# A two-block sequence model on one core: later places for three groups of matrix products in the mixers

## Chip, core and metric

The kernel runs on 1 core of one Trainium2 chip. The metric is the device time of one execution in microseconds; lower is better.

## What is computed

Two blocks on a sequence of 256 tokens of width 1024. Only the first part of the first block matters here, its two mixers and the merge behind them:

```python
hn = rms_norm(h, norm_mix_pre)
p_rw, p_ret, g_rw, g_ret = _split(hn @ w_in, IN_SIZES)
y_rw  = rwkv7_mixer(p_rw, ...)      # 8 heads of 64, a state per head, sequential over the tokens
y_ret = retention_mixer(p_ret, positions)   # q, k rotated; v, gate; chunks of 128 tokens
merged = sigmoid(g_rw) * (y_rw @ w_branch_rw) + sigmoid(g_ret) * (y_ret @ w_branch_ret)
h = h + rms_norm(merged @ w_out, norm_mix_post)
```

In the recurrent mixer r, k, v, a decay and a gate come from projections of `hn` that are mixed with the previous token. k is normalised per head (`kk / max(sqrt(sum(kk*kk)), 1e-12)`), and the state takes one step per token. In the retention mixer q and k go through a rotary embedding, a group norm per head follows, and the result is multiplied by `silu(g)`.

## The kernel before

All products with a weight matrix are made in fp32 from a high and a low part: `mm3` (L257) issues three MATMULs (L258 to L260) for each pair of tiles. A weight tile of 128x1024 comes by DMA into one of 3 `raw` buffers; ScalarE (ACT) writes the high part `whi` (L254), VectorE (DVE) the low part `wlo` (L255). Both have 3 buffers (tag `w`), so a split waits until TensorE (PE) has used the weight three places before it.

`weave` (L130) runs two generators by turns: for every `yield` of the main one, `ratio` steps of the side one. The main one is `ret_qk`, `ret_vg`, `gates(0, 4)` (L825): the retention mixer and the first gates. Its projections (`gemm_a_block`, L525) yield after each 6 MATMULs of 128x512. The side one is `mixer` (L820): `features` (L434), with `RATIO0` = 1.2 steps per yield of the main one, then `rwkv` (L628) with 0.6.

`features` makes four features f = 0 to 3 of the recurrent mixer, two heads each, in 7 steps. `rw_feature(i, out)` (L394) is one projection: 24 MATMULs of 128x256, then an ACTIVATE (L403) and a DVE operation (L404). For one feature:

- `rw_feature(4 + f, km)` gives k. ACT scales and squares it (L442, L443); two small products and Tanh (L448, L449) give the decay, a scan (L452) its running sum.
- *norm step* (L455 to L464): two products with a 128x2 constant (L457) sum the squares, DVE (L459), POOL (`pow`, L296) and ACT (L461) make the factors `rn`, ACT two exponentials `e2`, `cs` (L462, L463).
- *key step* (L466 to L480): PE turns `rn` (L468), and a chain on DVE, with ACT's L471 and L472 in it, writes the two halves of `KB` (L469, L470, L473, L474, four of L478 and L479). `rw_feature(f, rm)` is issued behind it.
- *Gram step*: r times decay into `KR` (L482), 8 products `KB` x `KR` (L487), masked by DVE into `Gm` (L490), three transposes (L494).
- `rw_feature(8 + f, vm)`, then transposes of v (L503 to L505), ones-product of r*k (L512), bonus (L513).

`rwkv` first inverts four triangular matrices at once (`inverse`, L603; products L598, masked copies on DVE L618, L619), then goes through 4 chunks of 64 tokens; after chunks 1 and 3 a group norm follows (L694 to L704, again with `pow` on POOL), then transposes (L708), a product for the gate (L712) and the split of the result `yrT`.

`ret_vg` (L722) ends in `gated` (L781): a projection of 48 MATMULs, then for both token tiles t Tanh (ACT L789), two DVE operations (L790, L791) and four transposes (L285) into `ytT`. The merge loop (L859) makes, for each of 8 output tiles f, 24 MATMULs with `ytT` and 12 with `yrT`.

The sequence of the Python text isn't yet that of the engines: the framework's list scheduler orders the instructions of each engine at build time, by the text's order and by when it expects each to be ready. At run time each engine takes its instructions strictly in that order.

Of the kernel before, what the change touches and what calls it, by code (L numbers as in the profile page):

```python
# [114 lines left out]
YR, PB0, PB2, PA0, PA2 = 1, 2, 1, 2, 1  # L115
QL0, QL1, QL2 = 3, 1, 4

RATIO0, RATIO1, RATIO2, RATIO3, RATIO4, RATIO5, RATIO6 = 1.2, 0.6, 0.8, 0.55, 0.75, 0.8, 0.5


@with_exitstack
def tile_block(ctx: ExitStack, tc: tile.TileContext, io):
# [39 lines left out]
    def sm():  # L162
        return tl(qp, [P, 512], "sm", 4)
# [15 lines left out]
    def PR(name):  # L179
        lo, hi = PAR[name]  # L180
        return par[:, lo:hi]
# [212 lines left out]
    def rw_feature(i, out):  # L394

        ps = mm()
        if len(w_first) == 3:
            gemm_b_passes(ps[:, :T], w_first.pop(0), xT)
        else:
            gemm_b(ps[:, :T], w_first.pop(0) if w_first else rw.next(), xT)  # L400
        m = u2()
        G.memset(m[:, 0:1], 0.0)
        S.activation(out=m[:, 1:T + 1], in_=ps[:, :T], func=AF.Identity, scale=PR("mu")[:, i:i + 1])  # L403
        V.scalar_tensor_tensor(out=out, in0=ps[:, :T], scalar=omu[:, i:i + 1], in1=m[:, 0:T], op0=mult, op1=add)  # L404
# [20 lines left out]
    def c4(ap):  # L425
        return ap.rearrange("p (c l) -> p c l", c=4)
# [7 lines left out]
    def features():  # L434
        for f in range(4):
# [1 line left out]
            km, rm = duo()  # L437
            vm = bonus[f]
            rw_feature(4 + f, km)
            yield  # L440
            kk, sq = duo()
            S.activation(out=kk, in_=km, func=AF.Identity, scale=PR("kk")[:, fs])  # L442
            S.activation(out=sq, in_=kk, func=AF.Square)  # L443
# [8 lines left out]
            V.tensor_tensor_scan(out=cs, data0=C("scan64"), data1=ld, initial=0.0, op0=mult, op1=add)  # L452
            rn = ld
            yield
            pn = sm()  # L455
            for t in range(2):
                PE.matmul(pn[:, 2 * t:2 * t + 2], sq[:, t * P:(t + 1) * P], C("heads2"), start=True, stop=True)  # L457
# [4 lines left out]
            S.activation(out=e2, in_=cs, func=AF.Exp, scale=-1.0)  # L462
            S.activation(out=cs, in_=cs, func=AF.Exp)  # L463
            V.tensor_copy(out=PL[:, f, :], in_=c4(cs)[:, :, 63])  # L464
            yield
            pn = sm()  # L466
            for t in range(2):
# [8 lines left out]
            for x in range(2):  # L476
                b = slice(64 * x, 64 * x + 64)
                V.scalar_tensor_tensor(out=KB[b, :, 1 - x, :], in0=c4(kk)[b], scalar=0.5, in1=c4(e2)[b], op0=mult, op1=mult)  # L478
                V.tensor_tensor(out=KB[b, :, x, :], in0=c4(km)[b], in1=c4(e2)[b], op=mult)  # L479
            rw_feature(f, rm)  # L480
            yield
            V.tensor_tensor(out=KR[f][:, :, 1, :], in0=c4(rm), in1=c4(cs), op=mult)  # L482
            pgs = [sm(), sm()]
            for c in range(4):

# [8 lines left out]
                PE.transpose(pk[:, c * P:(c + 1) * P], KB[:, c].rearrange("p a l -> p (a l)"), ident)  # L494
            S.activation(out=KBn[:, f], in_=pk[:, 0:384].rearrange("p (c l) -> p c l", c=3), func=AF.Copy)
            yield
            rw_feature(8 + f, vm)
            yield


            pv, pw0 = sm(), sm()
# [5 lines left out]
            S.activation(out=VU[0:64, f, :, 0:64], in_=pv[0:64].rearrange("p (c l) -> p c l", c=4)[:, :, 0:64], func=AF.Copy)  # L507
            S.activation(out=VU[64:128, f, 1:4, 64:128], in_=pv3[64:128, :, 64:128], func=AF.Copy)
            S.activation(out=VU[64:128, f, 0, 64:128], in_=pw0[64:128, 0:64], func=AF.Copy)
            V.scalar_tensor_tensor(out=rm, in0=rm, scalar=PR("rk")[:, fs], in1=km, op0=mult, op1=mult)  # L510
            pb = sm()
            PE.matmul(pb[:, 0:T], C("ones2"), rm, start=True, stop=True)  # L512
            V.tensor_tensor(out=vm, in0=pb[:, 0:T], in1=vm, op=mult)  # L513
# [208 lines left out]
    def ret_vg():  # L722
# [58 lines left out]
        def gated():  # L781
            for b in range(2):
                outs = [mm(), mm()]
                yield from gemm_a_block(ret, xT, outs)
                while len(ocs) < 2:
                    yield
                for t in range(2):
                    th, z = ru(), ocs[t][:, b * 512:(b + 1) * 512]
                    S.activation(out=th, in_=outs[t], func=AF.Tanh, scale=0.5)  # L789
                    V.scalar_tensor_tensor(out=th, in0=th, scalar=1.0, in1=outs[t], op0=add, op1=mult)  # L790
                    V.tensor_tensor(out=z, in0=z, in1=th, op=mult)  # L791
                    transposes(z, 4, ytT, t, 4 * b)
                    yield
        yield from woven(gated(), outputs(), RATIO2)

# [26 lines left out]
        ratio[0] = RATIO1  # L822
        yield from rwkv()

    weave(chain(ret_qk(), ret_vg(), gates(0, 4)), mixer(), ratio)  # L825

    def down(acc, w, xT, k, first, last, ts=(0, 1)):

# [31 lines left out]
    pend = None  # L860
    for f in range(KD + 1):
        if f < KD:
            pb = mm()
            br, bt = halves(pb)
            wt_, wr_ = w_br.next(), w_br.next()
            gemm_b(bt, wt_, ytT)
            gemm_b(br, wr_, yrT, nk=4)
            tg = tgs[f]
            V.scalar_tensor_tensor(out=tg, in0=tg, scalar=1.0, in1=pb, op0=add, op1=mult)
            mf = tl(p1, [P, T], "Pn", 3)  # L870
            V.tensor_tensor(out=mf, in0=tg[:, 0:T], in1=tg[:, T:2 * T], op=add)
            if f < 4:
                mg = tl(p1, [P, 2, T], "qkT", 4, F32R)
            else:
                if f == 4:
                    kbn = tl(p1, [P, 4, 3, P], "KBn", 1, F32R).rearrange("p f c l -> p (f c l)")
                    bon = [tl(p1, [P, T], f"bonus{x}", 1, F32R) for x in range(2)]
                mg = kbn[:, (f - 4) * 512:(f - 3) * 512].rearrange("p (a l) -> p a l", a=2) if f < 7 else None
            mh, ml = (mg[:, 0, :], mg[:, 1, :]) if f < 7 else bon
            S.activation(out=mh, in_=mf, func=AF.Copy, scale=0.5)  # L880
            V.scalar_tensor_tensor(out=ml, in0=mf, scalar=0.5, in1=mh.bitcast(F32), op0=mult, op1=sub)
            for _ in gates(f + 4, min(f + 5, KD)):
                pass
            if EARLY <= f < EARLY + LATE1:
                w_late.append(w_l.next(spare[f - EARLY]))
        if pend is not None:
            k, x = pend
            if acc is None:
                acc = [[sm(), sm()], [sm(), sm()]]
            if k < KD - LATE1:  # L890
                down(acc, w_o.next(), x, k, k == 0, False)
            else:
                late.append((w_late[k - KD + LATE1], x, False))
        if f < KD:
            pend = (f, (mh, ml))
# [754 lines left out]
```

## Time and profile before

| | |
|---|---|
| runs (3) | 891.41, 894.54, 895.50 us, median 894.54 |
| the profiled execution | 894.72 us, its span 893.0 us |
| granted TensorE clock | 0.997 of full speed over the span |
| PE, DVE, ACT, POOL busy | 859.5, 649.8, 519.3, 70.7 us |

Reading it: the span goes from the first to the last instruction. PE means the MATMULs; their ends are modelled, so a row of busy PE can hide a fraction of a microsecond of waiting. An idle time in brackets behind a row, with an arrow, names what ended it. DMA moved 144 MB.

### The profile page before, as it was taken

The page shows a single profiled execution, that of the slowest core. Times are in us where ns is not written, and L with a number is a line of the kernel's source. Part 1 is how long each engine was busy: PE and PEld are TensorE (multiplying, and loading weights), DVE is VectorE, ACT ScalarE, POOL GpSimd, SP SyncE. Part 2 cuts the span into 40 slices and gives each one's busy share as a digit, 9 for nine tenths or more (in the row PEclk, how much of TensorE's full clock was granted, in tenths as well). Part 3 has the DMA queues.
Part 4 walks back from the last instruction along what each step waited for, and adds up shares of the span by engine and source line. Part 5 has one row for each costly group of instructions (what it writes and reads, how often), then busy time and mean ns, then how long its engine had stood idle before and what let it go on. Part 6 is the DMA issues. An engine that isn't in the chain of part 4 may idle for free.

```text
span 893.0 us, 15886 instructions
## 1 busy us (share of the span) xinstructions
PE 859.5 (96%) x6226; PEld 750.0 (84%) x6226; DVE 649.8 (73%) x1117; ACT 519.3 (58%) x933; POOL 70.7 (8%) x105
## 2 busy tenths in 40 slices
PE   9999999999999999999999899999999999999997
PEld 6788788789898889989999689978887888878776
DVE  7778865774755777888788848878786569867643
ACT  6555533454554556665566646668676467756652
POOL 2000000100100100000000100001101002402000
PEclk9999999999999999999999999999999999999999
DMA  8432431334566476655556435654534458543311
GB/s 278 144 136 99 130 131 66 105 105 147 172 218 207 165 243 215 226 180 197 188 177 207 150 103 200 226 201 146 189 120 140 160 175 285 171 170 108 116 36 36
DMA packets 41996, 144.44 MB, mean 162 GB/s; under 512 B 4977, under 2 KB 5569, under 8 KB 41922
## 3 DMA queue, kind: packets, MB, share of 16 engines
q1 hardware_dynamic: 41312, 141.32, 47.2%
q0 software_dynamic: 608, 2.11, 0.8%
q8 instruction: 49, 0.80, 0.4%
q14 instruction: 25, 0.20, 0.1%
q10 hardware_dynamic: 2, 0.00, 0.0%
HBM read 140.24 MB, written 3.18 MB: 161 GB/s over the span
## 4 chain that ended last, share of the span: by engine, by line
PE 39%; issue 22%; DVE 15%; DMA 14%; ACT 7%; POOL 3%; ACTq 0%; POOLq 0%; DVEq 0%; SPq 0%
PE mm L260 9%; PE mm L258 9%; PE mm L259 9%; DMA raw<-in_w_down 8%; DVE wlo L255 3%; PE sm L598 3%; ACT lhi L254 2%; DMA raw<-in_w_br 2%; DVE llo L255 2%; DMA raw<-in_w_up 1%; PE sm L285 1%; PE sm L1521 1%; ACT whi L254 1%; DVE elo L255 1%; POOL sg L1180 1%
## 5 line engine op out<-in xcount | busy, mean ns | idle before, releaser
L254 ACT ACTIVATE whi<-raw 128x1024 fp32r<-128x1024 f32 (+1 forms) x125 | 128.4, 1029 | 114.6 <-PE mm L259 38.4
L255 DVE TENSOR_TENSOR wlo<-raw,whi 128x1024 fp32r<-128x1024 f32 (+1 forms) x124 | 146.5, 1185 | 56.2 <-ACT whi L254 54.0
L258 PE MATMUL mm<-xTh,whi 128*128 128x256 f32 x616 | 174.8, 284 | 0.2 <-ACT xTh L254 0.2
L259 PE MATMUL mm<-xTl,whi 128*128 128x256 f32 x616 | 174.0, 283 | 0.3 <-DVE xTl L255 0.3
L260 PE MATMUL mm<-xTh,wlo 128*128 128x256 f32 x616 | 173.6, 282 | 0.4 <-DVE wlo L255 0.4
L259 PEld LDWEIGHTS mm<-xTl,whi 128*128 128x128 f32 x616 | 116.5, 189 | 2.4 <-issue 0.7
L258 PEld LDWEIGHTS mm<-xTh,whi 128*128 128x128 f32 x616 | 116.3, 189 | 2.3 <-ACT xTh L254 0.5
L260 PEld LDWEIGHTS mm<-xTh,wlo 128*128 128x128 f32 x616 | 116.2, 189 | 1.3 <-DVE wlo L255 0.9
L258 PE MATMUL mm<-whi,xTh 128*128 128x512 f32 x168 | 68.3, 407 | 0.0
L260 PE MATMUL mm<-whi,xTl 128*128 128x512 f32 x168 | 67.4, 401 | 0.0
L259 PE MATMUL mm<-wlo,xTh 128*128 128x512 f32 x168 | 66.1, 394 | 0.0
L258 PE MATMUL mm<-lhi,xTh 128*128 128x512 f32 (+1 forms) x156 | 61.4, 394 | 2.4 <-DVE xs L1064 1.9
L260 PE MATMUL mm<-lhi,xTl 128*128 128x512 f32 (+1 forms) x156 | 61.0, 392 | 0.0
L259 PE MATMUL mm<-llo,xTh 128*128 128x512 f32 (+1 forms) x156 | 60.2, 386 | 0.0
L255 DVE TENSOR_TENSOR llo<-raw,lhi 128x1024 fp32r<-128x1024 f32 x38 | 47.3, 1246 | 16.2 <-ACT lhi L254 15.7
L254 ACT ACTIVATE lhi<-raw 128x1024 fp32r<-128x1024 f32 x38 | 40.0, 1057 | 25.7 <-DMA raw<-in_w_down 16.9
L990 DVE SCALAR_TENSOR_TENSOR fc<-mm,par,fc 128x255 f32<-128x255 f32 x88 | 41.9, 477 | 7.8 <-ACT fc L987 7.3
L260 PE MATMUL mm<-xTh,elo 128*128 128x256 f32 x168 | 47.3, 281 | 0.0
L259 PE MATMUL mm<-xTl,ehi 128*128 128x256 f32 x168 | 47.3, 281 | 0.0
L258 PE MATMUL mm<-xTh,ehi 128*128 128x256 f32 x168 | 47.3, 281 | 0.0
L987 ACT ACTIVATE fc<-mm,par 128x256 f32<-128x256 f32 x44 | 24.3, 553 | 23.6 <-DVE fc L990 23.6
L990 DVE SCALAR_TENSOR_TENSOR cv<-mm,par,cv 128x255 f32<-128x255 f32 (+2 forms) x72 | 34.2, 475 | 4.7 <-ACT cv L987 4.0
(482 smaller groups left out, 2024.6 us busy)
## 6 DMA issues: line engine op xcount, KB each, us to landing
raw<-in_w_up SPq DMA_DIRECT2D x44, 512.0 KB, 4.0
raw<-in_w_xbc SPq DMA_DIRECT2D x25, 512.0 KB, 3.9
raw<-in_w_ret SPq DMA_DIRECT2D x24, 512.0 KB, 3.6
raw<-in_w_down SPq DMA_DIRECT2D x22, 512.0 KB, 4.6
raw<-in_w_gate SPq DMA_DIRECT2D x16, 512.0 KB, 3.5
raw<-in_w_z SPq DMA_DIRECT2D x16, 512.0 KB, 4.1
raw<-in_w_so SPq DMA_DIRECT2D x16, 512.0 KB, 4.4
raw<-in_w_pg SPq DMA_DIRECT2D x16, 512.0 KB, 4.3
```

Of the source, the lines that this page charges most:

```text
L254: first = S.activation(out=hi, in_=src, func=AF.Copy)
L255: last_split[:] = first.ins, (eng or V).tensor_tensor(out=lo, in0=src, in1=hi.bitcast(F32), op=sub).ins
L258: PE.matmul(out, sh, mh, start=start, stop=False)
L259: PE.matmul(out, sh, ml, start=False, stop=False)
L260: return PE.matmul(out, sl, mh, start=False, stop=stop).ins
L285: last = PE.transpose(ps[:, i, :], src[:, (j + i) * P:(j + i + 1) * P], ident)
L598: PE.matmul(fv(px)[u, f, :], lhsT(f, x), rhs[u, f, :], start=True, stop=True)
L987: S.activation(out=c, in_=ps, func=AF.Identity, scale=wv[:, (ntap - 1) * nf + i:(ntap - 1) * nf + i + 1], bias=bv[:, i:i + 1])
L990: V.scalar_tensor_tensor(out=c[:, d:], in0=ps[:, :T - d], scalar=wv[:, j:j + 1], in1=c[:, d:], op0=mult, op1=add)
L1180: G.affine_select(out=sg, in_=sg, pattern=[[0, 8], [1, P]], compare_op=ALU.is_ge, fill=NEG, base=0, channel_multiplier=-1)
L1521: PE.matmul(po[:, o:o + 64], eT[:, j * P:(j + 1) * P], vn[kb][:, kv * 64:(kv + 1) * 64], start=(kb == 0), stop=(kb == nk - 1))
```

## The change

In `features` the steps are cut anew. `rw_feature(f, rm)` moves from behind the key step to a step of its own behind the scan, ahead of the norm step. `rw_feature(8 + f, vm)` moves from behind the Gram step to the end of the key step. L482 (now L466) goes into the norm step, the product for the bonus (L510, now L483) into the key step. An empty step (a second `yield`) stands between norm and key step; a feature has 8 steps in place of 7, and `RATIO0` goes from 1.2 to 1.37. In `gated` the transposes come one `yield` after the DVE operations of both token tiles. A new generator `first_branches` puts the 24 `ytT` products of the first two merged tiles at the end of the main generator; the merge loop then adds their 12 `yrT` products. No instruction is added or taken away in these stages.

```diff
@@ -115,7 +115,7 @@
 YR, PB0, PB2, PA0, PA2 = 1, 2, 1, 2, 1
 QL0, QL1, QL2 = 3, 1, 4
 
-RATIO0, RATIO1, RATIO2, RATIO3, RATIO4, RATIO5, RATIO6 = 1.2, 0.6, 0.8, 0.55, 0.75, 0.8, 0.5
+RATIO0, RATIO1, RATIO2, RATIO3, RATIO4, RATIO5, RATIO6 = 1.37, 0.6, 0.8, 0.55, 0.75, 0.8, 0.5
 
 
 @with_exitstack
@@ -437,7 +437,6 @@
             km, rm = duo()
             vm = bonus[f]
             rw_feature(4 + f, km)
-            yield
             kk, sq = duo()
             S.activation(out=kk, in_=km, func=AF.Identity, scale=PR("kk")[:, fs])
             S.activation(out=sq, in_=kk, func=AF.Square)
@@ -452,6 +451,8 @@
             V.tensor_tensor_scan(out=cs, data0=C("scan64"), data1=ld, initial=0.0, op0=mult, op1=add)
             rn = ld
             yield
+            rw_feature(f, rm)
+            yield
             pn = sm()
             for t in range(2):
                 PE.matmul(pn[:, 2 * t:2 * t + 2], sq[:, t * P:(t + 1) * P], C("heads2"), start=True, stop=True)
@@ -462,6 +463,8 @@
             S.activation(out=e2, in_=cs, func=AF.Exp, scale=-1.0)
             S.activation(out=cs, in_=cs, func=AF.Exp)
             V.tensor_copy(out=PL[:, f, :], in_=c4(cs)[:, :, 63])
+            V.tensor_tensor(out=KR[f][:, :, 1, :], in0=c4(rm), in1=c4(cs), op=mult)
+            yield
             yield
             pn = sm()
             for t in range(2):
@@ -477,9 +480,9 @@
                 b = slice(64 * x, 64 * x + 64)
                 V.scalar_tensor_tensor(out=KB[b, :, 1 - x, :], in0=c4(kk)[b], scalar=0.5, in1=c4(e2)[b], op0=mult, op1=mult)
                 V.tensor_tensor(out=KB[b, :, x, :], in0=c4(km)[b], in1=c4(e2)[b], op=mult)
-            rw_feature(f, rm)
-            yield
-            V.tensor_tensor(out=KR[f][:, :, 1, :], in0=c4(rm), in1=c4(cs), op=mult)
+            V.scalar_tensor_tensor(out=rm, in0=rm, scalar=PR("rk")[:, fs], in1=km, op0=mult, op1=mult)
+            rw_feature(8 + f, vm)
+            yield
             pgs = [sm(), sm()]
             for c in range(4):
 
@@ -494,8 +497,6 @@
                 PE.transpose(pk[:, c * P:(c + 1) * P], KB[:, c].rearrange("p a l -> p (a l)"), ident)
             S.activation(out=KBn[:, f], in_=pk[:, 0:384].rearrange("p (c l) -> p c l", c=3), func=AF.Copy)
             yield
-            rw_feature(8 + f, vm)
-            yield
 
 
             pv, pw0 = sm(), sm()
@@ -507,7 +508,6 @@
             S.activation(out=VU[0:64, f, :, 0:64], in_=pv[0:64].rearrange("p (c l) -> p c l", c=4)[:, :, 0:64], func=AF.Copy)
             S.activation(out=VU[64:128, f, 1:4, 64:128], in_=pv3[64:128, :, 64:128], func=AF.Copy)
             S.activation(out=VU[64:128, f, 0, 64:128], in_=pw0[64:128, 0:64], func=AF.Copy)
-            V.scalar_tensor_tensor(out=rm, in0=rm, scalar=PR("rk")[:, fs], in1=km, op0=mult, op1=mult)
             pb = sm()
             PE.matmul(pb[:, 0:T], C("ones2"), rm, start=True, stop=True)
             V.tensor_tensor(out=vm, in0=pb[:, 0:T], in1=vm, op=mult)
@@ -784,12 +784,16 @@
                 yield from gemm_a_block(ret, xT, outs)
                 while len(ocs) < 2:
                     yield
+                zs = []
                 for t in range(2):
                     th, z = ru(), ocs[t][:, b * 512:(b + 1) * 512]
                     S.activation(out=th, in_=outs[t], func=AF.Tanh, scale=0.5)
                     V.scalar_tensor_tensor(out=th, in0=th, scalar=1.0, in1=outs[t], op0=add, op1=mult)
                     V.tensor_tensor(out=z, in0=z, in1=th, op=mult)
-                    transposes(z, 4, ytT, t, 4 * b)
+                    zs.append(z)
+                yield
+                for t in range(2):
+                    transposes(zs[t], 4, ytT, t, 4 * b)
                     yield
         yield from woven(gated(), outputs(), RATIO2)
 
@@ -822,7 +826,17 @@
         ratio[0] = RATIO1
         yield from rwkv()
 
-    weave(chain(ret_qk(), ret_vg(), gates(0, 4)), mixer(), ratio)
+    begun = []
+
+    def first_branches():
+
+        for _ in range(2):
+            pb, w = mm(), w_br.next()
+            gemm_b(halves(pb)[1], w, ytT)
+            begun.append((pb, w_br.next() if not begun else None))
+            yield
+
+    weave(chain(ret_qk(), ret_vg(), gates(0, 4), first_branches()), mixer(), ratio)
 
     def down(acc, w, xT, k, first, last, ts=(0, 1)):
 
@@ -860,11 +874,11 @@
     pend = None
     for f in range(KD + 1):
         if f < KD:
-            pb = mm()
+            pb, wr_ = begun.pop(0) if begun else (mm(), None)
             br, bt = halves(pb)
-            wt_, wr_ = w_br.next(), w_br.next()
-            gemm_b(bt, wt_, ytT)
-            gemm_b(br, wr_, yrT, nk=4)
+            if f >= 2:
+                gemm_b(bt, w_br.next(), ytT)
+            gemm_b(br, wr_ or w_br.next(), yrT, nk=4)
             tg = tgs[f]
             V.scalar_tensor_tensor(out=tg, in0=tg, scalar=1.0, in1=pb, op0=add, op1=mult)
             mf = tl(p1, [P, T], "Pn", 3)
```

Line numbers shift: L457 becomes L458, L459 L460, L461 L462, L468 L471, L469 L472, L471 L474, L472 L475, L474 L477, L478 L481, L479 L482, L487 L490, L490 L493, L494 L497, L495 L498, L503 to L505 L504 to L506.

**TensorE, feature 3, ahead of the Gram products.** `whi`, `wlo` with 128x512 are retention projections, with 128x256 the features' (`rw_feature`). Before:

```order
L258 MATMUL mm<-whi,xTh 128x512
L259 MATMUL mm<-wlo,xTh 128x512
L260 MATMUL mm<-whi,xTl 128x512
L258 MATMUL mm<-whi,xTh 128x512
L260 MATMUL mm<-xTh,wlo 128x256
L487 MATMUL sm<-KR_261,u 128x128 x8
L494 MATMUL sm<-cst,u 128x128 x3
```

Now, from the turning of `rn` (L471) on:

```order
L471 MATMUL sm<-cst,u 128x128 x2
L260 MATMUL mm<-xTh,wlo 128x256
L258 MATMUL mm<-xTh,whi 128x256
L259 MATMUL mm<-xTl,whi 128x256
L260 MATMUL mm<-xTh,wlo 128x256
L577 MATMUL mm<-cst,kn_272 128x128 x4
L490 MATMUL sm<-KR_261,u 128x128 x8
L497 MATMUL sm<-cst,u 128x128 x3
L504 MATMUL sm<-cst,bonus_268 128x128 x3
L505 MATMUL sm<-cst,bonus_268 64x64
L506 MATMUL sm<-cst,bonus_268 64x64
```

Before, 11 MATMULs of 128x256 and 16 of 128x512 stand between the turning of `rn` and the Gram products of this feature; now 4 of 128x256 and 4 transposes of the retention (L577). In feature 1 it is likewise: before 25 of 128x256, 10 of 128x512 and 4 of L577, now 7 of 128x256 and 4 of L577. In features 0 and 2 there are now 18 and 11 of 128x256, each with 8 of 128x512. Over the stages of the change TensorE goes 97 times from a weight product to another kind or back, 91 times before.

**ScalarE, feature 3, around the copy into `KR`** (L474, before L471), the last thing on ACT that DVE's chain to `KB` waits for. Before:

```order
L461 ACTIVATE u_1045<-sm_nr_1077 128x256
L463 ACTIVATE u_1049<-u_1049 128x256
L472 ACTIVATE u_1045<-u_1045,der_162 128x256
L471 ACTIVATE KR3_261<-u_1038 128x4
L254 ACTIVATE whi_1172<-raw_1170 128x1024
```

Now:

```order
L254 ACTIVATE whi_1316<-raw_1314 128x1024
L462 ACTIVATE u_1017<-sm_nr_1067 128x256
L475 ACTIVATE u_1017<-u_1017,der_162 128x256
L254 ACTIVATE whi_1378<-raw_1376 128x1024
L474 ACTIVATE KR3_261<-u_1010 128x4
L579 ACTIVATE qkT_1137<-mm_1132 128x512
```

A weight split, `whi_1378`, now stands ahead of the copy; its buffer is that of the weight of the 4 MATMULs shown above behind L471, so it waits for them.

**TensorE, end of the recurrent mixer** (L708 turns its last normed tile). Before:

```order
L259 MATMUL mm<-xTl,whi 128x256
L260 MATMUL mm<-xTh,wlo 128x256
L708 MATMUL sm<-cst,u 128x128 x4
L712 MATMUL sm<-wagd,u 128x128 x4
L258 MATMUL mm<-xTh,whi 128x256
```

Now:

```order
L259 MATMUL mm<-xTl,whi 128x256
L260 MATMUL mm<-xTh,wlo 128x256
L708 MATMUL sm<-cst,u 128x128 x4
L712 MATMUL sm<-wagd,u 128x128 x4
L258 MATMUL mm<-ytTh,whi 128x256
```

Between the last output products of the chunks (L688) and L708 stand 72 MATMULs of 128x256 where 48 stood; behind L712 come the 48 `ytT` products of the first two merged tiles, of which 24 stood ahead of L708.

## Rows read from the trace of the kernel before

**Rows 1.** The page's first part: busy time, share of the span and instructions of each engine.

```profile
PE 859.5 (96%) x6226; PEld 750.0 (84%) x6226; DVE 649.8 (73%) x1117; ACT 519.3 (58%) x933; POOL 70.7 (8%) x105
```

**Rows 2.** Busy time by stage: the features, inverse and first chunks, later chunks with the end of the retention, merge. Columns: stretch, length, busy us (instructions) of PE, PEld, DVE, ACT, POOL, then granted clock, DMA share, GB/s.

```profile
20.00:108.00 88.00, 83.06 (x565) 70.33 (x563) 70.70 (x148) 50.05 (x92) 5.55 (x15) 1.00 0.40 135
108.00:176.00 68.00, 68.00 (x964) 56.79 (x964) 45.19 (x88) 27.14 (x49) 3.64 (x2) 1.00 0.28 95
176.00:229.00 53.00, 49.31 (x554) 45.53 (x553) 33.60 (x54) 24.59 (x37) 4.29 (x2) 1.00 0.39 130
229.00:260.00 31.00, 31.00 (x239) 29.92 (x238) 20.32 (x28) 16.54 (x25) 0.00 (x0) 1.00 0.58 196
```

**Rows 3.** Who TensorE waited for in the first 230 us: total us, times, longest.

```profile
PE sm L708 <- DVE u L704: 2.6, 2, 1.8
PE sm L468 <- ACT u L461: 2.4, 4, 0.7
...
PE sm L457 <- ACT u L443: 1.4, 1, 1.4
PE sm L285 <- DVE b L791: 1.1, 1, 1.1
...
PE sm L503 <- DVE bonus L404: 1.0, 2, 0.8
```

**Rows 4.** Timeline of TensorE, feature 0: start, us, instruction, in brackets the idle time before it. The first two rows are a change from weight products to others, the last four give the spacing of the products (128x256, then 128x512).

```profile
23.71 0.39 PE L260 MATMUL mm<-whi,xTl 128*128 128x512 f32 x1
24.03 0.48 PE L445 MATMUL sm<-wagd,u 64*128 64x256 f32 x1
...
28.22 0.61 PE L457 MATMUL sm<-cst,u 128*128 128x2 f32 x4 [1.44 <-ACT u L443]
30.94 0.44 PE L468 MATMUL sm<-cst,u 128*128 128x128 f32 x2 [0.62 <-ACT u L461]
...
33.14 0.28 PE L260 MATMUL mm<-xTh,wlo 128*128 128x256 f32 x1
33.26 0.28 PE L258 MATMUL mm<-xTh,whi 128*128 128x256 f32 x1
...
33.62 0.40 PE L258 MATMUL mm<-whi,xTh 128*128 128x512 f32 x1
33.85 0.40 PE L259 MATMUL mm<-wlo,xTh 128*128 128x512 f32 x1
```

**Rows 5.** Groups of DVE and ACT over 20 to 110 us: busy us, mean ns of one, idle before them.

```profile
L255 DVE TENSOR_TENSOR wlo<-raw,whi 128x1024 fp32r<-128x1024 f32 x22 | 26.8, 1219 | 6.6 <-ACT whi L254 6.6
L404 DVE SCALAR_TENSOR_TENSOR u<-mm,der,u 128x256 f32<-128x256 f32 x8 | 3.8, 480 | 0.1
...
L254 ACT ACTIVATE whi<-raw 128x1024 fp32r<-128x1024 f32 x22 | 23.2, 1057 | 15.4 <-PE mm L259 11.5 <-issue 2.1 <-PE mm L260 1.3
```

**Rows 6.** Timeline of feature 3's key step: TensorE's turn of `rn`, then DVE's chain up to the last half of `KB`.

```profile
94.86 0.44 PE L468 MATMUL sm<-cst,u 128*128 128x128 f32 x2 [0.49 <-ACT u L461]
...
95.33 0.42 DVE L469 TENSOR_TENSOR u<-sm,u 128x256 f32<-128x256 f32 x1
95.79 0.42 DVE L470 TENSOR_TENSOR KR<-u 128x252 f32<-128x252 f32 x1
96.13 0.42 DVE L473 TENSOR_TENSOR u<-u 128x256 f32<-128x256 f32 x1
96.46 0.42 DVE L474 SCALAR_TENSOR_TENSOR u<-u 128x256 f32<-128x256 f32 x1
96.80 0.41 DVE L479 TENSOR_TENSOR u<-u 64x256 f32<-64x256 f32 x1
97.13 0.85 DVE L478 SCALAR_TENSOR_TENSOR u<-u 64x256 f32<-64x256 f32 x2
97.90 0.42 DVE L479 TENSOR_TENSOR u<-u 64x256 f32<-64x256 f32 x1
```

**Rows 7.** The inverse: 32 products (x64 instructions) on TensorE, and DVE's masked copies behind the round before.

```profile
115.83 2.08 PE L598 MATMUL sm<-u,Gm 64*64 64x64 f32 x64
...
114.09 0.77 DVE L618 COPY_PREDICATED u<-msk,sm 128x256 f32<-128x256 uint8 x2
```

**Rows 8.** The last group norm of the recurrent mixer: its last products on TensorE, then ACT, DVE and POOL up to the transposes.

```profile
218.97 1.15 PE L688 MATMUL sm<-VU,Gm 128*64 128x64 f32 x32
...
227.84 0.63 PE L708 MATMUL sm<-cst,u 128*128 128x128 f32 x4 [1.79 <-DVE u L704]
...
221.55 0.76 DVE L697 TENSOR_TENSOR u<-sm,sm_gmu 128x256 f32<-128x256 f32 x2
...
223.36 0.68 DVE L702 TENSOR_REDUCE sm_grs<-u 128x8 f32<-128x512 f32 x1
...
227.00 0.69 DVE L704 TENSOR_TENSOR u<-u,sm_grs 128x512 f32<-128x512 f32 x1 [1.53 <-POOL sm_grs L296]
...
222.34 0.63 ACT L700 ACTIVATE u<-u 128x512 f32<-128x512 f32 x1 [1.11 <-DVE u L697]
```

**Rows 9.** All `pow` operations of POOL over 20 to 230 us: busy us, mean ns of one.

```profile
L296 POOL TENSOR_TENSOR sm_nr<-sm_nr,mhalf 128x4 f32<-128x4 f32 x4 | 4.7, 1186 | 58.0 <-DVE sm_nr L459 58.0
L296 POOL TENSOR_TENSOR sm_grs<-sm_grs,mhalf 128x8 f32<-128x8 f32 x2 | 4.3, 2144 | 47.8 <-DVE sm_grs L294 47.8
L296 POOL TENSOR_TENSOR sm_rva<-sm_rva,mhalf 128x8 f32<-128x8 f32 x2 | 3.6, 1822 | 76.8 <-DVE sm_rva L294 76.8
```

## The prediction

> **What bounds the kernel now.** First the busy times [rows 1]: TensorE 96% of the span, so only its idle time and its amount of work count, and the change leaves the amount alone. Then the stages [rows 2]: it is idle for 88.00 - 83.06 = 4.9 us in the features, 0 in the inverse, 3.7 near the end of the mixers, 0 in the merge. Then the waits [rows 3]: L457 1.4, four times L468 together 2.4, L503 1.0; later L285 1.1, and L708 twice, 2.6. These 8.5 us are all the change can win here, 0.95% of the time; 0.5% (4.5 us) is about what a measurement of this kernel can tell from no change. DVE works 70.7 of 88 us in the features [rows 2], so what is moved behind less cover soon waits for DVE.
>
> A weight product takes a place every 0.12 us at 128x256 (33.14 to 33.26) and 0.23 us at 128x512 [rows 4]; this is how I count cover. Where each wait stands now, and what it waits for, is from the order of the changed kernel; lengths are the trace's.
>
> **a. Waits for the squares and for v: -2.4.** L457 came right behind k's projection and waited 1.44 us for two ACT operations [rows 4]; now the 24 products of `rw_feature(f, rm)` stand between. L503 waited twice, 1.0 together [rows 3], for v's DVE step; v's products now stand a Gram step earlier. In none of the four features do I find these waits again.
>
> **b. The wait for the key's norm: 2.4 to 1.75, -0.6.** From L457 to L468 in feature 0 pass 30.94 - 28.22 = 2.7 us [rows 4]: DVE, POOL, ACT, and TensorE waits at the end. The new cover, with 0.5 for the small products: feature 0 0.5 + 6 x 0.23 + 6 x 0.12 = 2.6, feature 1 0.5 + 17 x 0.12 = 2.5, feature 2 3.4, feature 3 2.9. That would nearly do. But in features 0 to 2 DVE has a weight split and r's L404 ahead of L460, and ACT the `whi` part ahead of r's L403. The `whi` waits for the last of r's products, some 1.4 us ahead of L458: -1.4 + 1.06 + 1.22 + 0.48 [rows 5] = 1.3 us behind it, where L460 could have run at 0.65. The chain ends 0.7 later, at 3.4. Waits: 0.75, 0.9, 0.1, 0.
>
> **c. The Gram products lose their cover: +4.1.** From the turn of `rn` at 94.86 to the end of the last half of `KB` at 97.90 + 0.42 pass 3.46 us, DVE alone, one operation every 0.34 [rows 6]. In features 0 and 2 the new cover is 18 x 0.12 + 8 x 0.23 = 4.0 and 3.2 us, with 0.4 for the turn itself: enough, as r's late L404 delays the turn too. In feature 1 the main generator stands at the rotation of q and has no weight product to give: 0.4 + 7 x 0.12 + 0.7 (transposes, switches) = 2.0. DVE takes one operation of the rotation in between: 3.46 + 0.34 = 3.8. The first three Gram products run on the first half of `KB` (0.4), so 1.4 is lost. In feature 3 (rotation of k) the cover is 1.6 us, and ACT has a weight split ahead of the copy into `KR`; it waits for products behind the turn: 1.0 + 1.06 [rows 5] + 0.2 for the copy = 2.3, then five DVE operations with 0.34 to 0.43 each = 4.1, less 0.3 for products on the first half: 2.2. Behind the Gram products now come at once the transposes of v, which need a PSUM buffer that ACT frees by two copies: 0.5 more in feature 3.
>
> *A rule weighed.* DVE's rows start 0.33 to 0.34 us apart where each lasts 0.42 [rows 6]: they overlap by 0.08. The Trainium skill, "VectorE: DVE Perf Modes", section "The DRAIN you can't avoid", says that the next operation doesn't start until the pipeline is empty, semaphores or not, and excepts those that need not be held. By the rule without its exception eight links would take 0.6 us more in features 1 and 3 each, and the forecast would be 1.3 higher, 898.0; the rows show the exception, and the sum goes by the rows.
>
> **d. The inverse: +0.3.** 32 products take 2.08 us, a pair of masked copies 0.77 on DVE [rows 7]. The second round now follows the first with no weight product between, and a weight split delays the first copies: 0.15 + 0.1.
>
> **e. Short waits in the chunks: +0.55.** 12 to 24 products between a chunk's steps become 4 to 6 in places; the copies behind them take some 0.4 us. Three places, 0.1, 0.15 and 0.3. Below, nothing; above, 1.2 (one weight split in front of one of them).
>
> **f. The three late waits: 3.7 to 3.3, -0.4.** `pow` on 8 columns took 1.82 and 2.14 in the mean [rows 9]; I take 2.0. *L285*: the first pair of z is finished on DVE behind an operation that waits for the other tile's `pow`: from the products ahead, a split pair until 2.4, four operations until 4.3, `pow` until 6.3, two operations until 7.1. The cover is 0.5 + 22 x 0.23 = 5.6: 1.5 in place of 1.1. *First L708*: two steps of the gated block stand ahead of its `pow` on DVE. `pow` starts 1.6 us behind the last 128x512 product, L704 ends at 4.4; the cover is 26 x 0.12 = 3.1: 1.3 in place of 0.8. *Second L708*: before, from L688 at 218.97 to the end of L704, 8.7 us [rows 8]. Now a weight split stands between L697 and L700 or L702 and waits until 24 products behind L688 are through: 4.1 + 1.06 + 0.63 + 0.6 + 0.8 us [rows 5, 8], `pow` from 7.4, with 2.0 and 0.7 ready at 10.2. The cover is 1.0 + 72 x 0.12 = 9.6: 0.6 in place of 1.8. The 48 products behind L712 (5.7 us) cover the split of `yrT`, which costs nothing before either. Were the cover gone, 2 us of ACT and DVE would show.
>
> **g. Switches: +0.5.** Six more changes from a weight product to another kind or back; I take 0.1 each: behind the product at 23.71 the next would start at 23.94, and the first of another kind starts at 24.03 [rows 4]. Below 0, above 1.
>
> DMA: the 16 queues' share is 0.4 or less here [rows 2]; the issues keep their kind and number and only change order. Nothing is priced.
>
> **Sum.** -2.4 - 0.6 + 4.1 + 0.3 + 0.55 - 0.4 + 0.5 = +2.05, made against the profiled execution's own 894.72 (span 893.0 and 1.7 around it; the median of the runs is 0.2 lower): **896.7 us**.
>
> **Rivals.**
> *The covers hold (faster).* The splits on DVE and ACT come early enough that b, c, d fall to nothing and L285 and the first L708 are covered: -2.4 - 2.4 + 0.55 - 1.9 - 1.2 + 0.5 = -6.9, so 888. For it: every step was given 24 products behind its chain. Against: 3.46 us [rows 6] against 2.0 and 1.6 of cover.
> *The weight ring feeds back (slower).* A split waits for TensorE three weights back, and stands on DVE ahead of the next link of a chain, so a wait of TensorE delays the split that delays the next wait. If that costs each feature one more split (1.15), +4.6: 901. It decides if L460 starts over 1.3 us behind L458 in all four features; I have it so in three, by 0.7. For it: ACT's idle time ahead of L254 ends mostly with a product of TensorE (11.5 of 15.4 us) [rows 5]. Against: TensorE waits for no `wlo` now [rows 3].
> *The change does not do what it says.* In features 1 and 3 no weight product stands behind the chain; if the same holds for time elsewhere, old waits only change names: 894.7.
>
> **Chances.** Forecast 0.58, covers hold 0.14, ring 0.18, no effect 0.10. Faster by over 0.5% (below 890.1): 0.13, nearly all of the first rival. Slower by over 0.5% (above 899.0): 0.20, from the ring and the forecast's upper tail. Same: 0.67. Range 890.5 to 901.5: below it most of the first rival, above it part of the second; the bounds of c (nothing to 5.5), e, f (`pow` 1.6 to 2.65, times three) and g lie inside.
>
> **What would show it.** Right: L458 and L504 without waits; L471 with waits of 0.7 to 0.9 in features 0 and 1 only; a wait for DVE ahead of L490 in features 1 (1.4) and 3 (2.2), none in 0 and 2; three late waits of 1.5, 1.3, 0.6; the features' stage idle for 5.5 to 6.5 us in place of 4.9. Wrong: no wait ahead of L490 (then the first rival), or waits for `wlo` or in all four features (then the second).

## The result, and the profile after

The changed kernel took 900.08 us (median of 5 runs, 896.12 to 903.2) beside 894.54 of the kernel before. The ratio on record, which is not the quotient of the two medians, is 1.0058, 95% interval 1.0032 to 1.0085. Run again on another occasion the change came to 898.99, 1.0053 [1.0031, 1.0075]. Two runs of the study, one of this second series (906.93 us) and one of e1_features (909.61), were in a slower state of the chip: the medians count them, the ratios and clocks don't. The change makes the kernel about half a per cent slower. The forecast was 896.7, no change; the range (890.5 to 901.5) holds the time.

The profiled execution took 896.12 (span 894.4), only 1.4 above the profiled execution of before, and both had the same mean clock, 0.997. So the two profiles show where the change itself costs time. The same product of the merge's output projection starts here, first before, then after:

```profile
297.09 0.39 PE L259 MATMUL sm<-Gm,KBn 128*128 128x512 f32 x1
```

```profile
300.24 0.39 PE L259 MATMUL sm<-Gm,KBn 128*128 128x512 f32 x1
```

So the part of the program that was changed is 3.15 us longer, and what follows, whose text is the same, was 1.7 us shorter in this execution. Most of that is two waits for a weight, 0.5 us at 341 and 1.1 at 385, that only the trace of before has; a stretch at half clock (below) stands in both, at 590 us before and at 499 now.

Stages of the changed kernel, columns as in [rows 2]:

```profile
20.00:108.00 88.00, 81.38 (x554) 70.60 (x553) 68.15 (x144) 48.98 (x94) 5.29 (x15) 1.00 0.38 129
108.00:176.00 68.00, 67.92 (x982) 55.53 (x980) 44.94 (x87) 24.76 (x43) 1.64 (x1) 1.00 0.29 95
176.00:229.00 53.00, 51.18 (x531) 46.67 (x531) 36.11 (x63) 26.36 (x42) 4.91 (x3) 1.00 0.38 120
```

TensorE is idle for 6.6 us in the features (4.9 before) and 1.8 near the end of the mixers (3.7 before). Who it waited for from 20 to 300 us, columns as in [rows 3]:

```profile
PE sm L490 <- DVE u L481: 3.7, 2, 2.3
PE sm L471 <- ACT u L462: 2.4, 2, 1.7
PE mm L258 <- ACT whi L254: 1.5, 1, 1.5
PE sm L708 <- DVE u L704: 1.0, 1, 1.0
PE sm L285 <- DVE b L792: 0.8, 1, 0.8
PE mm L260 <- DVE wlo L255: 0.8, 1, 0.8
PE sm L512 <- ACT VU L509: 0.4, 1, 0.4
```

The waits for the squares and for v are gone, and a new one, L490 for `KB`, is the largest. The waits of the mixers sum to 8.4 us where they were 8.5: they changed names and grew longer one by one. The timeline of TensorE at the ends of the longest, and the Gram products:

```profile
33.95 0.44 PE L471 MATMUL sm<-cst,u 128*128 128x128 f32 x2 [1.67 <-ACT u L462]
38.30 1.69 PE L490 MATMUL sm<-KR,u 64*128 64x128 f32 x16
...
55.34 0.44 PE L471 MATMUL sm<-cst,u 128*128 128x128 f32 x2 [0.75 <-ACT u L462]
56.45 0.60 PE L577 MATMUL mm<-cst,ru 128*128 128x128 f32 x4
58.37 1.85 PE L490 MATMUL sm<-KR,u 64*128 64x128 f32 x16 [1.33 <-DVE u L481]
...
98.02 0.60 PE L577 MATMUL mm<-cst,kn 128*128 128x128 f32 x4
100.96 1.52 PE L490 MATMUL sm<-KR,u 64*128 64x128 f32 x16 [2.34 <-DVE u L481]
...
104.26 0.70 PE L512 MATMUL sm<-u,cst 128*128 128x256 f32 x2 [0.40 <-ACT VU L509]
```

The Gram products themselves take longer too. Before, features 0 and 3:

```profile
38.90 1.16 PE L487 MATMUL sm<-KR,u 64*128 64x128 f32 x16
...
100.35 1.16 PE L487 MATMUL sm<-KR,u 64*128 64x128 f32 x16
```

1.16 us has become 1.52 to 1.85 (the trace has two rows for each of the 8 MATMULs). From the first start to the last it is 0.89 in each feature before, and 1.42, 1.58, 1.24 and 1.24 now: 1.9 us for four features, which the prediction had no term for.

The granted clock is the third thing. Over the runs that are compared here its mean is 0.9955 for the kernel before (110 runs) and 0.9927 (standard error 0.0009) for the changed one (16). One straight line through the times of all 249 of these runs (a level for each kernel, one slope) gives 0.60 +- 0.05 us for 0.001 of the clock. The means of the times are 4.4 us apart; 1.7 of it goes with the clock, and 2.8 are left at equal clock. That is a relation between runs; it doesn't show by itself that the clock is the cause.

### The profile page after: what moved, and what is told of

Same layout as the page of the kernel before. It is cut to its first block, busy times and chain, and to the rows that moved or that the text cites. A ratio compares the mean times of both kernels' runs of the same rounds, so it can differ in the third digit from the quotient of the medians.

```text
span 894.4 us, 15886 instructions
## 1 busy us (share of the span) xinstructions
PE 861.1 (96%) x6226; PEld 751.0 (84%) x6226; DVE 651.0 (73%) x1117; ACT 518.7 (58%) x933; POOL 68.1 (8%) x105
## 4 chain that ended last, share of the span: by engine, by line
PE 44%; issue 17%; DMA 16%; DVE 12%; ACT 7%; POOL 3%; SPq 0%; ACTq 0%; POOLq 0%; DVEq 0%
PE mm L258 10%; PE mm L260 10%; PE mm L259 10%; DMA raw<-in_w_down 8%; PE sm L598 3%; DVE wlo L255 3%; DMA raw<-in_w_up 2%; ACT lhi L254 2%; ACT whi L254 1%; PE sm L285 1%; DVE llo L255 1%; PE sm L1535 1%; DMA sg<-acd 1%; DVE elo L255 1%; DMA raw<-in_w_out 1%
## 5 line engine op out<-in xcount | busy, mean ns | idle before, releaser
L255 DVE TENSOR_TENSOR wlo<-raw,whi 128x1024 fp32r<-128x1024 f32 (+1 forms) x124 | 147.2, 1191 | 63.4 <-ACT whi L254 60.5
L255 DVE TENSOR_TENSOR llo<-raw,lhi 128x1024 fp32r<-128x1024 f32 x38 | 47.3, 1247 | 13.8 <-ACT lhi L254 13.4
L258 PEld LDWEIGHTS mm<-whi,xTh 128*128 128x128 f32 x168 | 31.7, 189 | 8.0 <-issue 1.3
```

Source lines behind the costliest of these rows:

```text
L255: last_split[:] = first.ins, (eng or V).tensor_tensor(out=lo, in0=src, in1=hi.bitcast(F32), op=sub).ins
L258: PE.matmul(out, sh, mh, start=start, stop=False)
```

## The experiments

**Theory A**: the loss is made where the Gram and norm steps lost their cover. **Theory B**: a good part is a lower granted clock. Later **D**: the clock falls behind idle stretches of TensorE. **P**: the Gram products depend on the order of the two heads. Every ratio is to the kernel before on the same chip (medians 894.51 for e1 to e4, 894.46 for e5 to e8, 895.1 for e9 to e11, 895.52 for e12); the last column is the mean granted clock of the runs.

| run | what it is | median us | ratio, 95% | clock |
|---|---|---|---|---|
| e1_features | features' part | 902.31 | 1.0067 [1.0038, 1.0096] | 0.9929 |
| e2_late | two late edits | 900.29 | 1.0078 [1.0052, 1.0104] | 0.9945 |
| e3_again | the change again | 898.99 | 1.0053 [1.0031, 1.0075] | 0.9927 |
| e4_ratio | the change, RATIO0 1.2 | 898.67 | 1.0043 [1.0021, 1.0065] | 0.9948 |
| e5_yield | gated edit alone | 897.15 | 1.0024 [1.0004, 1.0045] | 0.9936 |
| e6_branch | early merge products alone | 895.61 | 1.0022 [0.9994, 1.0051] | 0.9953 |
| e7_cover | features, RATIO0 1.25 | 897.15 | 1.0024 [1.0000, 1.0047] | 0.9961 |
| e8_idle | before, longer waits | 900.23 | 1.0062 [1.0042, 1.0082] | 0.9932 |
| e9_halves | before, Gram by heads | 898.27 | 1.0031 [1.0008, 1.0053] | 0.9967 |
| e10_best120 | features, RATIO0 1.2, KB loop | 894.52 | 0.9994 [0.9973, 1.0015] | 0.9943 |
| e11_best115 | the same, 1.15 | 896.69 | 1.0020 [0.9998, 1.0042] | 0.9939 |
| e12_ratio1 | e10 with RATIO1 0.7 | 896.31 | 1.0016 [0.9995, 1.0036] | 0.9942 |

**The two parts.** e1_features is the diff without its hunks at `gated`, `first_branches` and the merge loop; e2_late is those hunks alone, with RATIO0 1.2.

> Only the part of the change in the four features (with its ratio 1.37); the end of the mixers as before. Theory A (cover): the loss is made here. The waits of the changed kernel come again, L471 about 2.4 us together and L490 about 3.7, none at L458 and L504, and the three late waits stay at 3.7: 3 to 4 us above the kernel before. Theory B (clock): a large share of the 5.5 us between the medians is a lower granted clock behind the mixers; then this kernel is 1 to 2 us above the kernel before where its clock is the same, and its runs part by their clocks.

> Only the two edits at the end of the mixers (transposes of the gated block one step later, products of the first two merged tiles ahead of the merge); the features as before with ratio 1.2. Theory A: these two gain. The second L708 waits 0 in place of 1.8, the first and L285 about what they did: 2 us below the kernel before. Theory B: as slow as the whole change for its lower clock, 2 us or more above the kernel before. If the late first weight (1.3 us at the start) belongs to the moved instructions of the features, it is not here; if it is chance, it may be.

e1_features shows L471 2.4 and L490 3.7 exactly as the whole change does, so these waits belong to the features' edit. Its excess is 6 us (0.0067 of 894.5), of which 1.6 go with the clock (0.9929 against 0.9955, at 0.60 for each 0.001). e2_late missed: the second L708 still waits, with 73 products of 128x256 ahead of it where the whole change, with 72, has no wait, and a wait is new:

```profile
PE sm L708 <- DVE u L704: 2.8, 2, 1.6
...
PE sm L258 <- ACT whi L254: 2.3, 1, 2.3
```

So the number of products ahead doesn't decide it alone. What differs is the work on DVE and POOL. In e2_late two weight splits (L255) run between L702 and the end of `pow`, the second begun just ahead of it (`Gm` serves as a weight's buffer here):

```profile
226.60 1.22 DVE L255 TENSOR_TENSOR Gm<-raw,Gm 128x1024 fp32r<-128x1024 f32 x1
227.73 0.17 DVE L294 TENSOR_SCALAR sm_grs<-sm_grs 128x8 f32<-128x8 f32 x1
227.80 1.22 DVE L255 TENSOR_TENSOR wlo<-raw,whi 128x1024 fp32r<-128x1024 f32 x1
227.97 2.54 POOL L296 TENSOR_TENSOR sm_grs<-sm_grs,mhalf 128x8 f32<-128x8 f32 x1 [38.45 <-DVE sm_grs L294]
```

In the changed kernel none does, and `pow` takes 0.9 us less:

```profile
222.13 1.64 POOL L296 TENSOR_TENSOR sm_grs<-sm_grs,mhalf 128x8 f32<-128x8 f32 x1 [27.90 <-DVE sm_grs L294]
```

In the kernel before, too, a split began just ahead of this `pow`:

```profile
224.25 1.23 DVE L255 TENSOR_TENSOR wlo<-raw,whi 128x1024 fp32r<-128x1024 f32 x1
224.32 2.65 POOL L296 TENSOR_TENSOR sm_grs<-sm_grs,mhalf 128x8 f32<-128x8 f32 x1 [34.15 <-DVE sm_grs L294]
```

Over the 14 profiles of the study `pow` on 8 columns took 2.54 to 2.65 in all 8 cases with a split begun just ahead of it. It took 1.64 in 37 others, also in the one where a split began 0.30 behind it (e11_best115), and 2.01 in the 11 that ran beside L791 (L792 in the kernels with the later transposes).

The late edits gain nothing by themselves. Of their 1.9 us in the whole change, 1.8 is this wait. It took both to end it, the 72 products and an order with no split beside `pow`: e1_features (37 products) and e5_yield (57) have `pow` at 1.64 too and still wait 1.4 and 1.6. Parts of an order do not add up: the parts cost 0.67 and 0.78%, the whole 0.55.

**The change again, and one number of it undone.**

> The changed kernel once more, for the spread of its times and clocks. Theory A: 3 to 4 us above the kernel before (3.1 at the end of the mixers in the profile), the rest of the 5.5 being spread. Theory B: 5 us or more again, with the clock at 0.99 in most runs. The wait of 0.6 for the first weight split at 18 us is chance by both: not in this profile, or not of that length.

> The whole change with one number undone: RATIO0 1.2 in place of 1.37. On TensorE the Gram products then have 4.3, 2.9, 3.2 and 4.3 us of weight products behind the turn of rn (by 0.12 and 0.23 us each) in place of 4.0, 0.8, 3.2 and 0.5, and the end of the mixers stands as in the kernel with the late edits alone. Theory A: no wait at L490 in features 0, 2, 3, at most 0.5 in feature 1; L471 waits 2.5 to 3.5 together; 3 us below the changed kernel, 1 to 2 below the one before. Rival (the moves as such cost: more switches, more queued splits, wherever the cover is): within 1 us of the changed kernel.

e3_again repeats 1.0053. Its profile has L471 (1.67, 0.75) and L490 (1.33, 2.34) to 0.01 us, and no wait at 18 us: what belongs to the order repeats, the late first weight was chance. It is worth 1.0 to 1.1 us: by so much the products behind 18.7 us start earlier in e3_again than in the first profile of the same kernel. e4_ratio, on TensorE's waits:

```profile
PE sm L708 <- DVE u L704: 3.5, 2, 2.3
PE mm L260 <- DVE wlo L255: 2.6, 3, 1.5
PE sm L258 <- ACT whi L254: 2.1, 1, 2.1
PE sm L471 <- ACT u L462: 1.0, 1, 1.0
...
PE mm L577 <- DVE ru L546: 0.9, 1, 0.9
PE sm L598 <- DVE u L609: 0.5, 2, 0.3
```

With cover given back, L490 no longer waits at all and the features' waits fall from 6.5 to 2.2: that is term c, shown. The time fell by only 0.1%, within the intervals: the end of the mixers now stands as in e2_late, with its waits of 2 us.

**The late edits one by one.**

> Only the transposes of the gated block one step later; features and merge as before. Theory A1: the wait of 2.3 us for a weight of the output projection, which the two late edits together showed in the merge, belongs to the early products of the merged tiles, so it is absent here; the waits at L285 and L708 sum to 3 to 4 us as before, time within 1.5 us of the kernel before. Rival: that wait comes from this edit; then it is here, 2 us above the kernel before.

> Only the products of the first two merged tiles ahead of the merge; features and gated block as before. Theory A1: the wait of 2 us or more for the output projection's weight in the merge is here, since the weights of the early products take places of the raw ring ahead of it; 2 to 4 us above the kernel before. Rival (it comes from the gated edit): no such wait, within 1 us of the kernel before.

A1 fell: neither shows the 2.3 us wait for the output projection's weight (e5_yield has 1.8 for another weight in the merge at 281 us, e6_branch 1.5 for two low parts). It takes both edits. Each alone costs 0 to 0.5%. Why e2_late's median is 5.8 us up while its own profile (895.56, the fastest of its runs) shows some 2 us is left open.

**Where the clock falls.** e8_idle adds to the kernel before

```diff
+            for _ in range(4):
+                V.tensor_scalar(out=xs[b], in0=xs[b], scalar1=1.0, scalar2=None, op0=mult)
             scaled = V.tensor_scalar(out=xs[b], in0=xs[b], scalar1=r, scalar2=None, op0=mult)
```

> The kernel before with four multiplications by 1 per half more in the chain that ends in xs (L944), ahead of the transposes that TensorE waits for at about 316, 507 and 664 us. The waits there grow by 1 to 3 us each. Theory D (each stretch of half clock follows an idle stretch of TensorE by 1 to 1.5 us, and a long idle stretch is followed by one more often): the mean granted clock falls to 0.993 or below, and behind the lengthened waits the profile shows half clock for 3.5 us. Rival (the clock falls at times of its own): mean clock 0.995 as before, and the time rises by the waits alone.

The waits of L285 for `xs` went from 3.6 to 7.8 us in the profile, nearly all of it in one, which grew from 1.07 to 5.63; the other two, expected to grow as well, did not. The mean clock fell from 0.9956 (34 runs of the kernel before on this chip) to 0.9932. That is for theory D and against the rival. The 4.2 us in the waits and 1.4 by the slope would make up the 5.5 measured (0.0062); that the whole 4.2 reaches the end is not shown, since TensorE has 2.4 us less of other waits at 341 to 387 us in this profile. Stretches at half clock (0.5 of 2.4 GHz is 1.2) with what stood ahead of them; columns as in [rows 2], the granted clock is the third number from the end. Before, behind an idle time of 1.94 us that ended at 590.0:

```profile
586.00:590.00 4.00, 2.06 (x11) 1.36 (x9) 3.80 (x6) 2.17 (x4) 0.00 (x0) 1.00 0.73 230
590.00:594.00 4.00, 4.00 (x12) 3.16 (x13) 2.29 (x5) 2.34 (x4) 0.00 (x0) 0.57 0.45 162
594.00:598.00 4.00, 4.00 (x21) 3.07 (x19) 3.83 (x6) 2.40 (x4) 0.00 (x0) 1.00 0.35 131
```

e1_features, behind the 2.34 us ahead of the Gram products of feature 3:

```profile
98.00:101.00 3.00, 0.90 (x11) 0.93 (x13) 2.87 (x9) 1.44 (x4) 0.00 (x0) 1.00 0.56 175
101.00:108.00 7.00, 6.60 (x29) 5.17 (x26) 6.37 (x13) 1.90 (x5) 0.00 (x0) 0.54 0.32 115
```

e8_idle, from the last microsecond of the 5.63 us on:

```profile
315.00:320.00 5.00, 0.00 (x0) 0.00 (x0) 4.35 (x12) 2.08 (x5) 3.14 (x2) 0.97 0.47 185
320.00:327.00 7.00, 6.38 (x29) 5.92 (x30) 5.67 (x7) 1.20 (x2) 0.05 (x1) 0.53 0.87 249
```

In the 14 profiles of the study, between 20 and 884 us, there are 21 such stretches, 16 of 3.4 us and 5 of 6.8; 17 come with an idle time of TensorE of 1.5 us or more (there are 53 of these), 4 with one of 0.7 to 1.5 us (of 159). Where TensorE was busy through one of 3.4 us, the products behind it start 1.4 to 1.6 us later than in an execution without it. The same wait is followed by one in one execution and not in the next: the 2.34 ahead of L490 in e1_features, but neither in the profile of the change nor in e3_again. Nor do long waits explain every difference of the mean clock: e11_best115 has two idle times of 1.5 us or more in its profile where the kernel before has three, and its clock is 0.9939 against 0.9957 on the same chip.

**The order of the heads.** e9_halves changes the kernel before in one place:

```diff
-            for c in range(4):
-                for x, b in enumerate(VH):
+            for x, b in enumerate(VH):
+                for c in range(4):
```

> The kernel before with the Gram products issued by halves (four of one head, then four of the other) in place of head by head in turn. Theory P (pairs): two products of 64 rows on different halves of the partitions run at the same time when they follow each other; the 16 passes of a feature start within 0.89 us before and take 1.25 to 1.59 us in the changed kernel, where the scheduler put three of one head first. By halves they take 1.6 to 1.8 us, 0.7 to 0.9 more for each feature, 3 to 3.5 us above the kernel before. Rival (the longer Gram stretch of the changed kernel is only the wait for the second half of KB): spacing stays 0.89, time within 1 us of the kernel before.

```profile
39.62 1.71 PE L487 MATMUL sm<-KR,u 64*128 64x128 f32 x16
```

The starts now spread over 1.41 to 1.44 us in each feature, 0.53 more (expected 0.7 to 0.9); the time is up by 0.31%, 2.8 us. With the heads in turn, the rows of a pair start 6 to 8 ns apart in three of the four features, and the pairs 0.11 us; of one head, every row takes 0.11. The Trainium skill, "TensorE: Matmul & The Clock Gate", Part 3, section "The mechanism", says that small products on different row groups of the array overlap, with starts some 4 ns apart; the trace agrees, at 6 to 8 ns. In the changed kernel the list scheduler put three products of one head first in features 0 and 1 (3, 3, 1, 1) and two in feature 3, presumably because it expected that head's half of `KB` earlier; in feature 2 the order alternates, and the late second half shifts the pairs.

**Towards a better version.** e7_cover is e1_features with RATIO0 1.25. e10_best120 has 1.2, and

```diff
-            for x in range(2):
-                b = slice(64 * x, 64 * x + 64)
+            for x, b in enumerate(VH):
                 V.scalar_tensor_tensor(out=KB[b, :, 1 - x, :], ...)
+            for x, b in enumerate(VH):
                 V.tensor_tensor(out=KB[b, :, x, :], ...)
```

e11_best115 is the same with 1.15; e12_ratio1 is e10_best120 with RATIO1 0.7.

> Only the features' part of the change, with RATIO0 1.25; the end of the mixers in its old text. On TensorE the Gram products have 4.0, 3.3, 3.6 and 4.3 us of weight products behind the turn of rn, and ahead of the first L708 stand 9.3 us in place of 6.0, ahead of L285 6.7 in place of 4.2. Theory A: no wait over 0.5 at L490, L285 and the first L708; L471 2 to 3 us together, the second L708 1 to 2: 3 to 4 us below the kernel before. Rival (the moves cost wherever the cover is, by switches and queued splits): within 1 us of the kernel before or above it.

> Only the features' part of the change, with RATIO0 1.2, and the four DVE operations of KB in another order (both halves of the one kind, then both of the other) so that all Gram products stand head by head in turn on TensorE. The end of the mixers is the old one. Theory A with P: L471 waits 1 us, the rotation's turns (L577) 1.2, the first products of the inverse 0.7; nothing at L490; the Gram products take 0.9 to 1.1 us; about 1.5 to 2 us below the kernel before. Rival (more changes between kinds of products and the standing waits eat the rest, as with ratio 1.25): at the kernel before or up to 2 us above.

> The same with RATIO0 1.15: every Gram step has 4.3 us of weight products behind the turn of rn, the norm steps 2.8, 1.4, 2.8 and 2.8. Theory A with P: no wait at L490; L471 0.5 to 1.5 us together; the other waits move with the place of the retention's steps, 3 to 5 us in all later; 1 to 3 us below the kernel before. Rival: within 1 us of it or above.

> The kernel with the features' part, RATIO0 1.2 and the turned loop over KB (e10_best120), and RATIO1 0.7 in place of 0.6, which sets how fast the recurrent mixer's chunks go beside the retention's. On TensorE the second L708 then has 72 weight products behind the chunks' last output, as in the changed kernel, where it waited 0; L285 has 22 products of 128x512, as there (0.8). Theory A: the late waits fall from 3.7 to 1.5 to 2.5 together, the waits of the features stay, 1 to 2 us below e10_best120, so 2 to 3 below the kernel before. Rival (cover in the inverse becomes thinner for it, or a weight's split takes the place): as e10_best120 or slower.

e7_cover: no wait at L490, as A said; but L285 and the first L708 still waited 1.0 and 1.4 with 6.7 and 9.3 us of products ahead, and L471 3.3. There the rival was right: 1.0024, not 3 to 4 us below. e10_best120 has this left:

```profile
PE sm L708 <- DVE u L704: 2.6, 2, 1.8
PE sm L285 <- DVE b L791: 1.1, 1, 1.1
PE sm L471 <- ACT u L462: 1.0, 1, 1.0
PE mm L577 <- DVE ru L546: 0.9, 1, 0.9
```

It is the only one not above the kernel before (0.9994), and 0.6% under the change; but its interval holds no gain. The turned loop did not shorten the Gram stretch (1.50 us in the row of feature 0, as in e4_ratio, which has the old loop), so the expected 0.9 to 1.1 missed, and by that the gain over e1_features goes to the ratio. e11_best115 has no wait at L490 and 1.0 at L471, as A said, and in features 1 to 3 its Gram products start within 0.89 to 0.97 us; but it waits 2.3 us at the turns of the rotation (L577) and 0.8 at L512, and its 1.0020 is on the rival's side. e12_ratio1 brought the late waits from 3.7 to 2.0, as A said, and paid with

```profile
PE mm L260 <- DVE wlo L255: 3.5, 4, 1.5
```

in the merge, 0.8 in e10_best120; at 1.0016 the rival held there as well. No version beats the kernel before clearly.

## Why the prediction came out as it did

The range held, and term c was right in place and size. The sum of the terms, +2.05, also comes near what the two profiles show for them, about +2.0; but that is luck: b, d with e, f and g missed by 0.3 to 1.5 us, and a term of 1.9 was missing. The time was 3.4 us above the forecast all the same; the sum had no term for the clock, with which 1.7 us go, and the rest lies in chance and in what is open below. The rival "the covers hold" is refuted by L490. The rival of the weight ring fails by its own sign: L460 starts 2.6, 1.5, 1.3 and 0.8 us behind L458, not over 1.3 in all four features, and no wait for `wlo` came into the mixers. The sum's terms, as measured in the profile:

- **a, -2.4**: right. L458 and L504 do not wait.
- **b, -0.6**: 0. The wait at this place was 2.4 us before and is 2.4 now. L471 waited 1.67 and 0.75 where 0.75 and 0.9 were forecast. I had the `whi` split of feature 0 wait for TensorE; it waited for ACT itself, which loads a table just before (it did so in the kernel before, too) and was late. ACT, then DVE:

```profile
27.23 1.28 ACT L447 ACT_TABLE_LOAD   x1
28.52 0.47 ACT L447 ACTIVATE u<-sm,der 128x256 f32<-128x256 f32 x1
...
29.56 1.06 ACT L254 ACTIVATE whi<-raw 128x1024 fp32r<-128x1024 f32 x1
```

```profile
30.65 1.23 DVE L255 TENSOR_TENSOR wlo<-raw,whi 128x1024 fp32r<-128x1024 f32 x1 [0.59 <-ACT whi L254]
31.79 0.48 DVE L404 SCALAR_TENSOR_TENSOR u<-mm,der,u 128x256 f32<-128x256 f32 x1
32.19 0.15 DVE L460 TENSOR_SCALAR sm_nr<-sm 128x4 f32<-128x4 f32 x1
```

  L458 starts at 29.56, so L460 runs 2.6 us behind it, not 1.3. The chain of one feature was walked, but with all engines taken as on time at its head.
- **c, +4.1**: 1.33 in feature 1, 2.34 in feature 3 and 0.48 behind (L506, L512) are 4.15 against 1.4 + 2.2 + 0.5. Right in place and size.
- **missing, +1.9**: the Gram products' own time. The term c counted them at their length of before, though the order, with the tiles' numbers, showed that the heads no longer alternate.
- **d, +0.3; e, +0.55**: 0.1 together. In the inverse and the first chunks TensorE is idle for 68.00 - 67.92 = 0.08 us, and all of its 1.8 us in the later chunks are L285 and L708.
- **f, -0.4**: -1.9 (the three waits forecast add to 3.4, not 3.3, so the term should have read -0.3). L285 0.8 (1.5 forecast), the first L708 1.0 (1.3), the second 0 (0.6). The mis-sized piece is `pow`, taken at 2.0: ahead of all three it took 1.64, with no split begun ahead of it on DVE, which is 1.1 of the 1.5 us.
- **g, +0.5**: 0.1 to 0.2 is what the rest leaves for the switches. Of the measured 3.15, the waits up to 229 us are -0.2, the Gram products 1.9, the late first weights 1.0 to 1.1 (with the same issues ahead of them; chance, see e3_again) and the merge 0.2 (its first weight, 1.5 in place of 1.3).

Waits by themselves: -0.2 (forecast +1.5). So the order costs some 2.0 us in the stages of the change and 0.2 in the merge, against 2.8 between the means at equal clock; the remaining 0.6 is open. The clock goes with another 1.7 us by the slope; the chances had no case in which more idle time of TensorE is paid a second time. The third rival was half right: time in waits did stay the same under other names.

What stays open: why the whole costs no more than each of its two parts alone, and what lowers the clock. The change adds two waits over 1.5 us (1.7 and 2.3) and takes one away (1.8). One more, by 17 in 53 and half of the 4.2 us that a stretch lasts in the mean, would lower the mean clock by 0.0008, and 0.0028 were measured.

## To carry to other kernels

Cover must be counted at the step that loses it, with the engines as late as they are when the step begins, and in time of the waiting engine, not in steps of a generator. When a schedule is changed, compare the order with buffer numbers too: the neighbours of small products decide whether they overlap. For a small operation on POOL, look at what DVE begins just ahead of it. Where one long idle time replaces several short ones, count it with more than its length.

## Not expected of the hardware

The granted clock fell to half around idle times of TensorE of 1.1 to 2.3 us (once 5.6), in about one of three of 1.5 us or more, and a stretch of 3.4 us cost 1.4 to 1.6 us. The mean granted clock differs between the kernels (0.9927 to 0.9967); that added idle time lowers it is shown by e8_idle alone (0.9956 to 0.9932). A `pow` of POOL on 128x8 took 1.64 us, and 2.54 to 2.65 where DVE had begun a weight split just ahead of it. Two fp32 products of 64 rows on the two halves of the partitions run side by side when they alternate: 0.89 us from the first start to the last for 16 rows, against 1.41 to 1.44 by halves.
